# A sixth seven-product unit in the second feed-forward layer of a two-layer encoder, units spread evenly, their first phase bank pair by bank pair, and one more raw and split weight buffer

## The chip, the cores and the metric

The kernel runs on one core of one Trainium2 chip. The metric is the device time of one execution in microseconds, as the median of several. TensorE (PE; its weight loads are PEld) multiplies, VectorE (DVE) and ScalarE (ACT) work element by element, GpSimd (POOL) here only issues DMAs that add, and SyncE (SP) issues the weight loads.

## The reference

Two encoder layers on x of 256 tokens x 2048 channels, all float32. The first has a mixer of pooling and grouped-query attention, the second a bidirectional mLSTM. Each is followed by the gated feed-forward part that this change is about:

```python
D_FF = 5632

def conv_ffn(x, w_up, conv_w, conv_b, w_down):
    u = x @ w_up                                  # 2048 -> 2 * D_FF
    up = jnp.pad(u, ((0, 0), (1, 1), (0, 0)))
    u = c[0] * up[:, :-2] + c[1] * up[:, 1:-1] + c[2] * up[:, 2:] + conv_b
    gate, val = jnp.split(u, 2, axis=-1)
    return (jax.nn.silu(gate) * val) @ w_down

x = x + conv_ffn(rms_norm(x, norm_ffn[layer]), w_up[layer], conv_w[layer], conv_b[layer], w_down[layer])
```

## The kernel before

**Weights as a stream.** All weights of the program stand in one list of chunks, mostly 128 x 1024 floats (512 KB). `Stream.load` has SP load chunk i into a raw tile `w{i}`. `Stream.split` makes a pair `hl{i}` of it: a cast to the rounded type by ScalarE (line 152) and the remainder by VectorE (line 153). TensorE then multiplies three times (high x high, high x low, low x high). Tiles come from pools of a fixed number of buffers, and chunk i + n waits in the queue of ScalarE until TensorE has let go of the buffer of chunk i. Inside a feed-forward layer there are `wraw` 6 + 1 raw and `wsplit` 4 + 1 split buffers (`home` gives every seventh or fifth chunk the extra one); `la` and `sa` say how many chunks ahead are loaded and split.

**A feed-forward layer.** The 44 feature tiles of 128 (each has a gate and a value half) are made in blocks c = 0 to 5 of 4, 8, 8, 8, 8 and 8 tiles (`FCH`). A plain tile `up` takes 4 chunks and 64 matmuls: 32 of 512 columns and 32 of 256. A *unit* makes four tiles at once: the product of 2 x 2 blocks (two halves of the tokens, two halves of a pair of weight rows) by seven products in place of eight, into four PSUM banks `p1`, `p5`, `p6`, `p4`. It takes 16 chunks in its first phase (8 weight quadrant sets p, each with a chunk for p1 and p5 and one for p6 and p4), then 8 chunks for p5 and p6 with one more for p1 after every second: 28 in all, and 7 x 8 x 3 matmuls of 512 columns. Then the banks are combined (lines 1047 to 1068: c12, c21, c22, c11), and `finish` transposes them back tile by tile (line 1081, four transposes a tile), at 3, 7, 11 and 15 us of the planner's clock after the unit's last chunk. `tail` does for every tile the convolution (lines 958 to 961), SiLU (964), the product with the value half (965), and writes the tile to `g` in a high part (966, ScalarE) and a low part (967, VectorE). The sums of weight quadrants that a unit needs are made ahead of time for kinds 1 to 3 by DMAs that add in DRAM (`make_step`, lines 121 to 128: two copies by SP and four accumulates by POOL for a quad of kind 2); the rest, and all of kind 0, are made by VectorE in `sums` (lines 140 to 146).

The down-projection `dn{layer}_{c}_{b}` multiplies block c's tiles in `g`, k = 0 to 7, two a chunk, with four column blocks b, and adds into x. Block c's down-projection is interleaved with block c + 1.

**What sets the order.** `UNITS` lists for each layer the units as (block, half, first slot, last slot, kind), and `_ffn_plan` lays their chunks between the slots of the plain tiles and of the down-projection. TensorE's order is this program order. ScalarE's, VectorE's and SP's come from a scheduler at build time; each queue is then fixed. `late` keeps a unit from taking its banks until the `finish` of the one before is written.

Of the kernel before, what the change touches and what calls it, by code (L numbers as in the profile page):

```python
# [16 lines left out]
P = 128  # L17
# [47 lines left out]
class Stream:  # L65
# [152 lines left out]


@with_exitstack  # L220
def trunk(ctx: ExitStack, tc: tile.TileContext, gx, xT, xn, call, catt, cml, weights, make, out):
# [239 lines left out]
    def attention_layer(norm, nxt):  # L461
        with ExitStack() as es:
# [475 lines left out]
    def ffn_layer(layer, norm, nxt):  # L938
        with ExitStack() as es:
# [76 lines left out]
            def sum_of(j, p):  # L1016
                return [sx[:, j, p, i, :] for i in range(2)]

            def quads(fs, c, i0, name):

                def bank(j):
                    return psp.tile([P, 512], F32, tag="ps", name=f"p{j}_{name}")

# [4 lines left out]
                r0, r1 = norm.rcol[:, 0:1], norm.rcol[:, 1:2]  # L1028
                for p in range(m):
                    ends = p == 0, p == m - 1  # L1030
                    if p == 0:
                        wv.until(lambda: not late)
                        late.update((0, 2))
                    hl = st.next()
                    if p == 0:
                        b1, b5 = bank(1), bank(5)
                    product(b1, block_of(2 * p, 0), hl, 0, *ends)
                    product(b5, sum_of(0, p), hl, 512, *ends)
                    yield
                    hl = st.next()  # L1040
                    if p == 0:
                        b6, b4 = bank(6), bank(4)
                    product(b6, sum_of(1, p), hl, 0, *ends)
                    product(b4, block_of(2 * p + 1, 1), hl, 512, *ends)
                    if p == m - 1:
                        c12, c21, c22 = part(12), part(21), part(22)
                        a.activation(c12, b1, AF.Copy, scale=n0)
                        a.activation(c21, b1, AF.Copy, scale=r1)
                        a.activation(c22, b5, AF.Copy, scale=r1)
                        v.scalar_tensor_tensor(c12, b6, n0, c12, ALU.mult, ALU.add)  # L1050
                    yield
# [22 lines left out]
            def finish(top, bottom, fs, gt, i0, name):  # L1074

                for n, f in enumerate(fs):
                    tr = psp.tile([P, 2, S], F32, tag="ps", name=f"tr{layer}_{f}")
                    for j in range(2):
# [67 lines left out]
            gts, run, late = {}, {}, set()  # L1146
            def g_of(c):
                if c not in gts:
                    gts[c] = actp.tile([P, 8, 2, S], F32R, tag=f"B{c % 2}", name=f"g{layer}_{c}")
                return gts[c]  # L1150

            for step in _ffn_plan(layer):
                kind, c = step[:2]
                key = step[:3]
                if key not in run:
                    f0 = sum(FCH[:c])
                    run[key] = (up(f0 + step[2], g_of(c), step[2]) if kind == "n" else
                                down(c, gts[c], step[2]) if kind == "d" else
                                quads([f0 + 4 * step[2] + j for j in range(4)], c, 4 * step[2], f"{layer}_{c}{step[2]}"))
# [3 lines left out]
            st.la, st.sa, st.more = 5, 2, None  # L1163

# [60 lines left out]
def _down_chunks(w):  # L1225
# [56 lines left out]
def _ffn_order(layer, up, dn, four, last):  # L1282
# [4 lines left out]
    for step in _ffn_plan(layer):  # L1287
# [7 lines left out]
        else:  # L1295
            u = [e[:2] for e in UNITS[layer]].index((c, i))
            made = UNITS[layer][u][4]
            if n >= 2 * m and (n - 2 * m) % 3 == 2:
                seq.append(last[u, (n - 2 * m) // 3])
                continue  # L1300
            at = n // 2 if n < 2 * m else (n - 2 * m) // 3 * 2 + (n - 2 * m) % 3
            q, key = four[u, at], f"{layer}{c}{i}_{at}"
            if n >= 2 * m:
                seq.append(("made", ((key, 1, 2), q[:, 1024:1536])) if made == 1 else ("left", q[:, 512:1536]))
            elif n % 2:
                seq.append(("made", ((key, 2, 4),)) if made in (1, 2) else ("chain", q[:, 1024:2048]))
# [127 lines left out]
```

## Time and profile before

| | |
|---|---|
| median of 3 runs | 2161.71 us (2161.03 to 2166.64) |
| profiled execution, span from first to last instruction | 2160.9 us |
| attention layer, until the first `up` | 256.4 us |
| first feed-forward layer | 712.3 us |
| mLSTM layer | 479.7 us |
| second feed-forward layer, 1448.4 to the last matmul | 708.2 us |
| TensorE busy | 2153.2 us |

The page gives no other time of the profiled execution than its span; the median of the runs stands 0.8 us above it, which is what lies around the span. The layers are cut where the chain in order of time shows their first and last matmuls. The shares of busy time on a page are averages: a stage with an idle engine beside one that is full is read from windows of the trace, and a wait from the row of the instruction that was late, which names in brackets how long its engine was idle and who ended it.

### The profile page before, as it was taken

What the parts mean: (1) busy time and instruction counts of PE and PEld (TensorE: products, weight loads), DVE (VectorE), ACT (ScalarE), POOL (GpSimd) and SP (SyncE); (2) the same over time, 40 slices, a digit from 0 to 9 for tenths busy, and PEclk for the clock granted to TensorE, in tenths of its full rate; (3) what the DMA queues carried; (4) which work ended last, traced back from release to release, by engine and by line L of the source; (5) the groups of instructions that cost most, each with busy time, mean ns of one, the idle gap of its engine ahead of it and who ended that gap; (6) DMA issues with size and microseconds to landing.
All of it is one profiled execution on the core that took longest, in us unless ns stands there. A gap on an engine that the chain in (4) does not pass through costs nothing.

```text
span 2160.9 us, 31049 instructions
## 1 busy us (share of the span) xinstructions
PE 2153.2 (100%) x10896; PEld 1826.7 (85%) x10896; DVE 1717.8 (79%) x2400; ACT 1309.2 (61%) x1840; POOL 276.0 (13%) x344
## 2 busy tenths in 40 slices
PE   9999999999999999999999999999999999999999
PEld 7888888888888888888888888888888888888887
DVE  7686698989889797866777677669898888879785
ACT  7665566766557576655454544556676666757663
POOL 0122111111111111111111111110000010000000
PEclk9999999999999999999999999999999999999999
DMA  8878899999999999979998998887999999877773
GB/s 325 257 229 246 256 262 345 316 332 320 308 325 308 351 332 339 319 200 250 250 263 251 256 253 244 258 244 223 312 286 306 302 297 288 272 249 238 259 245 119
DMA packets 204702, 596.15 MB, mean 276 GB/s; under 512 B 26010, under 2 KB 28354, under 8 KB 204546
## 3 DMA queue, kind: packets, MB, share of 16 engines
q1 hardware_dynamic: 167776, 531.43, 70.1%
q0 software_dynamic: 33696, 59.00, 18.3%
q10 hardware_dynamic: 3074, 3.75, 0.9%
q8 instruction: 85, 1.39, 0.2%
q14 instruction: 71, 0.58, 0.1%
HBM read 591.93 MB, written 119.58 MB: 329 GB/s over the span
## 4 chain that ended last, share of the span: by engine, by line
PE 93%; DMA 5%; DVE 1%; ACT 0%; issue 0%; SPq 0%; ACTq 0%; DVEq 0%
PE up L268 23%; PE dn L268 20%; PE p L268 16%; PE op L268 8%; PE mo L268 4%; PE mk L268 4%; PE mq L268 4%; PE mv L268 3%; PE qproj L268 3%; PE kproj L268 1%; PE vproj L268 1%; PE tr L1081 1%; DMA w<-G 1%; PE pool L268 1%; DMA w<-in_m_in 1%; DMA w<-in_up 1%
## 5 line engine op out<-in xcount | busy, mean ns | idle before, releaser
L153 DVE TENSOR_TENSOR hl<-w,hl 128x1024 fp32r<-128x1024 f32 (+2 forms) x892 | 1075.6, 1218 | 319.9 <-ACT hl L152 302.0
L152 ACT CAST hl<-w 128x1024 fp32r<-128x1024 f32 (+2 forms) x891 | 924.8, 1048 | 646.9 <-PE up L268 98.9
L268 PE MATMUL up<-xx,hl 128*128 128x512 f32 (+1 forms) x3072 | 560.2, 337 | 0.0
L268 PEld LDWEIGHTS up<-xx,hl 128*128 128x128 f32 x3072 | 486.7, 188 | 76.7
L268 PE MATMUL dn<-hl,g 128*128 128x512 f32 x2064 | 491.8, 391 | 0.0
L268 PEld LDWEIGHTS dn<-hl,g 128*128 128x128 f32 x2064 | 385.1, 188 | 79.0
L268 PE MATMUL p<-hl,sx 128*128 128x512 f32 x960 | 250.6, 390 | 0.0
L124 POOL DMA_DIRECT2D G<-in_q x160 | 132.0, 830 | 875.5 <-DMA G<-in_q 872.4
L268 PEld LDWEIGHTS p<-hl,sx 128*128 128x128 f32 x960 | 176.0, 188 | 34.4 <-DVE hl L153 0.6
L128 POOL DMA_DIRECT2D G<-G x144 | 127.9, 888 | 538.2 <-DMA G<-in_q 243.0
L268 PE MATMUL p<-hl,xx 128*128 128x512 f32 x720 | 193.5, 390 | 0.0
L268 PEld LDWEIGHTS p<-hl,xx 128*128 128x128 f32 x720 | 130.8, 188 | 24.0
L268 PE MATMUL mk<-xx,hl 128*128 128x512 f32 (+1 forms) x512 | 92.5, 338 | 1.4 <-DVE hl L153 1.4
L268 PE MATMUL mq<-xx,hl 128*128 128x512 f32 (+1 forms) x512 | 92.2, 337 | 0.0
L268 PE MATMUL mv<-hl,xx 128*128 128x512 f32 (+2 forms) x480 | 91.8, 350 | 0.0
L268 PE MATMUL op<-hl,cat 128*128 128x512 f32 x384 | 91.6, 393 | 0.0
L268 PE MATMUL mo<-hl,xx 128*128 128x512 f32 x384 | 90.5, 391 | 0.0
L268 PEld LDWEIGHTS mk<-xx,hl 128*128 128x128 f32 x512 | 79.0, 188 | 13.1 <-DVE hl L153 1.8
L268 PE MATMUL op<-hl,mcat 128*128 128x512 f32 x384 | 89.5, 392 | 0.0
L268 PEld LDWEIGHTS mq<-xx,hl 128*128 128x128 f32 x512 | 79.3, 188 | 11.6
L268 PEld LDWEIGHTS mv<-hl,xx 128*128 128x128 f32 x480 | 78.3, 189 | 11.2
L268 PEld LDWEIGHTS op<-hl,mcat 128*128 128x128 f32 x384 | 71.5, 188 | 14.6
(242 smaller groups left out, 1865.2 us busy)
## 6 DMA issues: line engine op xcount, KB each, us to landing
w<-in_up SPq DMA_DIRECT2D x192, 512.0 KB, 6.1
w<-in_dn SPq DMA_DIRECT2D x176, 512.0 KB, 6.2
w<-in_m_in SPq DMA_DIRECT2D x124, 512.0 KB, 6.0
w<-in_q SPq DMA_DIRECT2D x88, 512.0 KB, 6.2
G<-in_q SPq DMA_DIRECT2D x144, 256.0 KB, 6.4
G<-G POOLq DMA_DIRECT2D x144, 256.0 KB, 7.5
w<-G SPq DMA_DIRECT2D x72, 512.0 KB, 6.1
w<-in_a_in SPq DMA_DIRECT2D x46, 512.0 KB, 6.1
```

The costliest lines, as they stand in the source:

```text
L124: pin(add.dma_start(G[r, 0:512], src[r, 512:1024], accum_op=ALU.add))
L128: pin(add.dma_start(G[:, at : at + 512], G[:, of : of + 512], accum_op=ALU.add))
L152: (self.nc.vector.tensor_copy if i + c == 0 else self.nc.scalar.copy)(hl[:, 0, c : c + n], w[:, c : c + n])
L153: self.nc.vector.tensor_sub(hl[:, 1, c : c + n], w[:, c : c + n], hl[:, 0, c : c + n].bitcast(F32))
L268: pe.matmul(out_, lhsT, rhs, start=start, stop=stop, skip_group_check=True)
L1081: pe.transpose(tr[:, j, t * P : t * P + P], src[:, c : c + P], ident)
```

## The change

The second layer's block 3 has now both of its halves as units: (3, 0) is new, of kind 2. The six units there follow each other with a pause of 1.5 slots, where the five had pauses of 7 slots. From block 4 on, the plain tiles of a block come ahead of the down-projection of the block before. Units of kinds 1 and 2, in both layers, run all eight chunks of p1 and p5 first, then all eight of p6 and p4 (`apart`); the PSUM pool of four banks is two pools of two, with p1 and p5 on one side, and p6, p4 and the transposes on the other. Every raw and split pool has one more buffer, and `la` and `sa` are one higher everywhere; the DMA scratch of the program is 4096 bytes a partition to make room. The last 20 quads (they were 12) of the second layer are made 12 chunks apart, each within 15 chunks, instead of 17 apart and within 24.

```diff
     def home(self, i, raw):
-        return ((self.wpool if i % 7 < 6 else self.more[0]) if raw else
-                (self.spool if i % 5 < 4 else self.more[1]))
+        return ((self.wpool if i % 8 < 7 else self.more[0]) if raw else
+                (self.spool if i % 6 < 5 else self.more[1]))
...
+class Banks:
+    def __init__(self, *pools):
+        self.pools, self.n = pools, 0
+
+    def tile(self, shape, dtype, tag, name, side=None):
+        if side is None:
+            side = self.n % 2
+            self.n += 1
+        return self.pools[side].tile(shape, dtype, tag=tag, name=name)
...
-    wp = pool("wraw", 6)
-    sp = pool("wsplit", 4)
+    wp = pool("wraw", 7)
+    sp = pool("wsplit", 5)
...
-    psp = pool("ps", 4, space=PSUM)
+    psp = Banks(pool("ps", 2, space=PSUM), pool("pq", 2, space=PSUM))
...
-            st.sa = 2
+            st.la, st.sa = 6, 3
...
-                for p in range(m):
+                for q in range(2 * m):
+                    p, second = (q % m, q >= m) if apart else (q // 2, q % 2)
                     ends = p == 0, p == m - 1
-                    if p == 0:
+                    if q == (m if apart else 0):
                         wv.until(lambda: not late)
                         late.update((0, 2))
                     hl = st.next()
-                    if p == 0:
-                        b1, b5 = bank(1), bank(5)
-                    product(b1, block_of(2 * p, 0), hl, 0, *ends)
-                    product(b5, sum_of(0, p), hl, 512, *ends)
-                    yield
-                    hl = st.next()
+                    if not second:
+                        if p == 0:
+                            b1, b5 = bank(1), bank(5)
+                        product(b1, block_of(2 * p, 0), hl, 0, *ends)
+                        product(b5, sum_of(0, p), hl, 512, *ends)
+                        yield
+                        continue
...
-            st.la, st.sa, st.more = 7, 3, (lp(f"fw{layer}", 1), lp(f"fh{layer}", 1), st.at + len(_ffn_plan(layer)))
+            st.la, st.sa, st.more = 8, 4, (lp(f"fw{layer}", 1), lp(f"fh{layer}", 1), st.at + len(_ffn_plan(layer)))
...
-    ((1, 1, 17, 39, 2), (2, 1, 46, 67, 2), (3, 1, 74, 97, 2), (4, 1, 104, 128, 2), (5, 1, 135, 157, 2)),
+    ((1, 1, 17, 37, 2), (2, 1, 38.5, 59, 2), (3, 0, 60.5, 80, 2), (3, 1, 81.5, 99, 2), (4, 1, 100.5, 123, 2),
+     (5, 1, 124.5, 146, 2)),
...
+            if c > 3 and len(UNITS[layer]) > 5:
+                fill.sort(key=lambda e: e[0] == "d")
...
-    nc = _bacc.Bacc("TRN2", target_bir_lowering=False, num_devices=1)
+    nc = _bacc.Bacc("TRN2", target_bir_lowering=False, num_devices=1, dynamic_dma_scratch_size=4096)
...
-                  + [(at + 17 * k, 8) for k in range(12)])
+                  + [(at + 12 * k, 5) for k in range(20)])
```

In the rows of the order that follow, `p1_1_41` is bank p1 of unit (4, 1) of the second layer, `dn1_3_0` the first column block of block 3's down-projection, `hl792` the split pair of chunk 792, `y1_25` and the cast to `g1_3` behind it feature tile 25, which is k = 5 of block 3 (24 is k = 4; both belong to unit (3, 1)). The changed file's lines stand 13 to 16 higher from `mm` on.

TensorE, before, at the begin of block 3's down-projection; k = 4 and 5 come with its third chunk, hl768:

```order
L268 MATMUL p6_1_41_17107<-hl763_17171,sx1_13321 128x512 x3
L268 MATMUL p4_1_41_17108<-hl763_17171,xx3_9017 128x512 x3
L268 MATMUL dn1_3_0_17240<-hl764_17182,g1_3_15913 128x512 x12
L268 MATMUL p1_1_41_17094<-hl765_17220,xx3_9017 128x512 x3
L268 MATMUL p5_1_41_17095<-hl765_17220,sx1_13321 128x512 x3
L268 MATMUL dn1_3_0_17240<-hl766_17231,g1_3_15913 128x512 x12
L268 MATMUL p6_1_41_17107<-hl767_17243,sx1_13321 128x512 x3
L268 MATMUL p4_1_41_17108<-hl767_17243,xx3_9017 128x512 x3
L268 MATMUL dn1_3_0_17240<-hl768_17261,g1_3_15913 128x512 x12
```

ScalarE, before, where tiles 24 and 25 are cast to g:

```order
L152 CAST hl761_17139<-w761_17064 128x1024
L966 CAST g1_3_15913<-y1_24_16990 128x256
L964 ACTIVATE y1_25_17043<-y1_25_17043 128x256
L152 CAST hl762_17150<-w762_17088 128x1024
L152 CAST hl763_17171<-w763_17102 128x1024
L966 CAST g1_3_15913<-y1_25_17043 128x256
L152 CAST hl764_17182<-w764_17115 128x1024
```

Both casts stood behind the casts of chunks up to hl763, five chunks ahead of hl768.

TensorE at the same place in the change; the third chunk is hl792:

```order
L281 MATMUL dn1_3_0_17629<-hl788_17540,g1_3_16484 128x512 x12
L281 MATMUL p1_1_41_17427<-hl789_17569,xx3_9029 128x512 x3
L281 MATMUL p5_1_41_17428<-hl789_17569,sx1_13332 128x512 x3
L281 MATMUL dn1_3_0_17629<-hl790_17609,g1_3_16484 128x512 x12
L281 MATMUL p1_1_41_17427<-hl791_17620,xx3_9029 128x512 x3
L281 MATMUL p5_1_41_17428<-hl791_17620,sx1_13332 128x512 x3
L281 MATMUL dn1_3_0_17629<-hl792_17632,g1_3_16484 128x512 x12
L281 MATMUL p6_1_41_17712<-hl793_17650,sx1_13332 128x512 x3
```

ScalarE in the change, where tiles 24 and 25 are cast to g:

```order
L152 CAST hl796_17692<-w796_17630 128x1024
L1062 ACTIVATE c12_1_41_17871<-p1_1_41_17427,n0_1_13333 128x512
L1063 ACTIVATE c21_1_41_17872<-p1_1_41_17427,re_n3_13411 128x512
L152 CAST hl797_17709<-w797_17647 128x1024
L1064 ACTIVATE c22_1_41_17873<-p5_1_41_17428,re_n3_13411 128x512
L971 ACTIVATE y1_25_17556<-tb_1_25_17554,cst_87 128x256 x2
L979 CAST g1_3_16484<-y1_24_17501 128x256
L971 ACTIVATE y1_31_17592<-tb_up1_31_17588,cst_87 128x256 x2
L977 ACTIVATE y1_25_17556<-y1_25_17556 128x256
L977 ACTIVATE y1_31_17592<-y1_31_17592 128x256
L979 CAST g1_3_16484<-y1_25_17556 128x256
```

The casts to g for hl792 stand now behind copies of p1 and p5, whose last first-phase products are hl791's, and behind the cast of hl797, five chunks past hl792. Split buffers are six in turn here (hl791 and hl797 have the same one) and were five before. VectorE in the change, at the end of that place:

```order
L153 TENSOR_TENSOR hl797_17709<-w797_17647,hl797_17709 128x1024
L972 SCALAR_TENSOR_TENSOR y1_25_17556<-tb_1_25_17554,cst_87,y1_25_17556 128x255 x2
L980 TENSOR_TENSOR g1_3_16484<-y1_24_17501,g1_3_16484 128x256
L974 SCALAR_TENSOR_TENSOR y1_25_17556<-tb_1_25_17554,cst_87,y1_25_17556 128x255 x2
L972 SCALAR_TENSOR_TENSOR y1_31_17592<-tb_up1_31_17588,cst_87,y1_31_17592 128x255 x2
L974 SCALAR_TENSOR_TENSOR y1_31_17592<-tb_up1_31_17588,cst_87,y1_31_17592 128x255
L978 TENSOR_TENSOR y1_25_17556<-y1_25_17556 128x256
L974 SCALAR_TENSOR_TENSOR y1_31_17592<-tb_up1_31_17588,cst_87,y1_31_17592 128x255
L978 TENSOR_TENSOR y1_31_17592<-y1_31_17592 128x256
L980 TENSOR_TENSOR g1_3_16484<-y1_25_17556,g1_3_16484 128x256
```

The low part of tile 25 has moved behind the split of hl797 and behind plain tile 31.

The second place is the last down-projection of the layer. TensorE in the change, where unit (5, 1) has ended and its last tile (41, k = 5) is transposed inside `dn1_5_0`'s first chunk:

```order
L281 MATMUL dn1_5_0_19336<-hl886_19232,g1_5_18134 128x512 x6
L1096 MATMUL tr1_41_19348<-cst_87,c11_1_51_19173 128x128
L1096 MATMUL tr1_41_19348<-cst_87,c21_1_51_18811 128x128
L1096 MATMUL tr1_41_19348<-cst_87,c11_1_51_19173 128x128
L1096 MATMUL tr1_41_19348<-cst_87,c21_1_51_18811 128x128
L281 MATMUL dn1_5_0_19336<-hl886_19232,g1_5_18134 128x512 x6
L281 MATMUL dn1_5_0_19336<-hl887_19249,g1_5_18134 128x512 x12
L281 MATMUL dn1_5_0_19336<-hl888_19284,g1_5_18134 128x512 x12
```

ScalarE behind these transposes, in the change:

```order
L1098 COPY tb_1_41_19353<-tr1_41_19348 128x512
L971 ACTIVATE y1_41_19355<-tb_1_41_19353,cst_87 128x256 x2
L152 CAST hl892_19391<-w892_19282 128x1024
L152 CAST hl893_19408<-w893_19317 128x1024
L977 ACTIVATE y1_41_19355<-y1_41_19355 128x256
L979 CAST g1_5_18134<-y1_41_19355 128x256
```

Before, a whole plain tile (39) and a column block of `dn1_4` stood between these transposes and `dn1_5_0`; now its third chunk, hl888, needs tile 41.

The third place is VectorE at the begin of the mLSTM layer, where `arg0` waits for a DMA through DRAM. Before:

```order
L153 TENSOR_TENSOR hl420_9471<-w420_9380,hl420_9471 128x1024
L801 COPY mc_9444<-cols_9439 128x8 x8
L829 SCALAR_TENSOR_TENSOR arg0_9578<-G0_9575,mc_9444,kml_9028 128x128
L829 SCALAR_TENSOR_TENSOR arg0_9578<-G0_9575,mc_9444,kml_9028 128x256 x2
L829 SCALAR_TENSOR_TENSOR arg0_9578<-G0_9575,mc_9444,kml_9028 128x128
```

In the change:

```order
L153 TENSOR_TENSOR hl421_9479<-w421_9388,hl421_9479 128x1024
L814 COPY mc_9456<-cols_9451 128x8 x8
L842 SCALAR_TENSOR_TENSOR arg0_9586<-G0_9583,mc_9456,kml_9040 128x128
L842 SCALAR_TENSOR_TENSOR arg0_9586<-G0_9583,mc_9456,kml_9040 128x256 x2
L842 SCALAR_TENSOR_TENSOR arg0_9586<-G0_9583,mc_9456,kml_9040 128x128
```

One split more stands ahead of it.

More of the change, by code (lines that the diff above doesn't have):

```diff
@@ L1017, in sum_of, with quads @@
                 return [sx[:, j, p, i, :] for i in range(2)]
-            def quads(fs, c, i0, name):
+            def quads(fs, c, i0, name, apart):
                 def bank(j):
-                    return psp.tile([P, 512], F32, tag="ps", name=f"p{j}_{name}")
+                    return psp.tile([P, 512], F32, tag="ps", name=f"p{j}_{name}", side=int(j in (1, 5)))
                 def part(j):
@@ L1076, in finish @@
                 for n, f in enumerate(fs):
-                    tr = psp.tile([P, 2, S], F32, tag="ps", name=f"tr{layer}_{f}")
+                    tr = psp.tile([P, 2, S], F32, tag="ps", name=f"tr{layer}_{f}", side=0)
                     for j in range(2):
@@ L1158, in ffn_layer @@
                                 down(c, gts[c], step[2]) if kind == "d" else
-                                quads([f0 + 4 * step[2] + j for j in range(4)], c, 4 * step[2], f"{layer}_{c}{step[2]}"))
+                                quads([f0 + 4 * step[2] + j for j in range(4)], c, 4 * step[2], f"{layer}_{c}{step[2]}",
+                                      (c, step[2]) in apart))
                 next(run[key], None)
@@ L1162, in ffn_layer @@
                 assert next(e, None) is None
-            st.la, st.sa, st.more = 5, 2, None
+            st.la, st.sa, st.more = 6, 3, None
     norms = [Norm(0), None]
@@ L1300, in _ffn_order @@
                 continue
-            at = n // 2 if n < 2 * m else (n - 2 * m) // 3 * 2 + (n - 2 * m) % 3
+            second = n >= m if made in (1, 2) else n % 2
+            at = (n - 2 * m) // 3 * 2 + (n - 2 * m) % 3 if n >= 2 * m else n % m if made in (1, 2) else n // 2
             q, key = four[u, at], f"{layer}{c}{i}_{at}"
```

3 lines of the change are left out of this document (2 added, 1 removed).

## The prediction

> **What bounds the kernel now.** I read the page first: engine totals, TensorE clock, shares of the chain.
>
> ```profile
> span 2160.9 us, 31049 instructions
> ...
> PE 2153.2 (100%) x10896; PEld 1826.7 (85%) x10896; DVE 1717.8 (79%) x2400; ACT 1309.2 (61%) x1840; POOL 276.0 (13%) x344
> ...
> PEclk9999999999999999999999999999999999999999
> ...
> PE 93%; DMA 5%; DVE 1%; ACT 0%; issue 0%; SPq 0%; ACTq 0%; DVEq 0%
> ```
>
> TensorE is busy all the time at its full clock, and the chain that ended last is 93% TensorE. So the time is the sum of TensorE's work, plus the places where it waits. Whether the second feed-forward layer has such places is read from the windows of the two layers (columns: stretch, its length, busy time of PE, PEld, DVE, ACT, POOL, granted clock, DMA share, GB/s).
>
> ```profile
> 1448.40:2156.60 708.20, 708.20 (x3523) 598.73 (x3521) 595.01 (x780) 444.38 (x577) 38.94 (x48) 1.00 0.82 262
> 256.40:968.70 712.30, 711.58 (x3548) 601.24 (x3547) 612.53 (x813) 456.90 (x604) 111.67 (x139) 1.00 0.99 312
> ```
>
> The second layer (first row) has no idle TensorE at all, though VectorE works 84% of it (595.01 of 708.20). A matmul removed there is a gain, if nothing that it covered comes late.
>
> **The change part by part. Matmuls.** Four `up` tiles give way to one unit. Two long stretches of the chain in order of time give the pace, and the groups by form show that `p` and `dn` matmuls are alike.
>
> ```profile
> 266.76 41.10 PE up L268 x236
> ...
> 2102.19 43.53 PE dn L268 x192
> ```
>
> ```profile
> L268 PE MATMUL dn<-hl,g 128*128 128x512 f32 x2064 | 491.8, 391 | 0.0
> ...
> L268 PE MATMUL p<-hl,sx 128*128 128x512 f32 x960 | 250.6, 390 | 0.0
> L268 PEld LDWEIGHTS p<-hl,sx 128*128 128x128 f32 x960 | 176.0, 188 | 34.4 <-DVE hl L153 0.6
> ```
>
> Removed: 4 x 64 matmuls at 41.10/236 = 0.174 us, 44.6 us. Added: 7 x 8 x 3 = 168 at 43.53/192 = 0.227 us, 38.1 us, and four groups of four transposes. A group in the timeline (start, length, what):
>
> ```profile
> 2084.95 0.60 PE L1081 MATMUL tr<-cst,c 128*128 128x128 f32 x4
> 2085.31 4.38 PE L268 MATMUL dn<-hl,g 128*128 128x512 f32 x18
> ```
>
> The next matmul starts 0.36 us after the transposes, and its row is 0.13 us longer than 17 spacings and one matmul of 0.39 (4.25): 0.5 us each, 1.9 us for four. Sum: 44.6 - 38.1 - 1.9 = **-4.6 us**.
>
> **VectorE and ScalarE.** A unit takes 28 weight chunks for the 16 of four `up` tiles, and 8 of them are summed first.
>
> ```profile
> L153 DVE TENSOR_TENSOR hl<-w,hl 128x1024 fp32r<-128x1024 f32 x882 | 1067.2, 1222 | 316.4 <-ACT hl L152 298.5 <-DMA G<-in_q 3.7 <-DMA w<-in_m_in 2.4
> L152 ACT CAST hl<-w 128x1024 fp32r<-128x1024 f32 x882 | 918.0, 1051 | 643.9 <-PE up L268 98.9 <-PE dn L268 93.2 <-DVE w L140 90.5
> ...
> L140 DVE TENSOR_TENSOR w<-w 128x512 f32<-128x512 f32 x80 | 54.8, 685 | 1.6 <-DMA w<-in_q 1.6
> ```
>
> VectorE gets 12 x 1.22 + 8 x 0.69 = 20.1 us more; the combining of banks it adds and the gathering of `up` it drops are within 2 us of each other. So about 615 us in 704: 87%, against 86% (612.53 of 712.30) in the first layer, which lost 0.7 us of TensorE. On average this is hidden; the question is where work that TensorE needs soon stands in the queue.
>
> **The wait at block 3's down-projection.** Here the order rows of the change decide. From unit (3,1)'s last chunk to the third chunk of `dn1_3_0` TensorE's rows, counted at the paces above, take 32 us now and took 49 before. In ScalarE's order the casts of g tiles 24 and 25, which `dn1_3_0` reads with chunk hl792, stand behind three copies that need unit (4,1)'s last first-phase products (chunk hl791) and behind the cast of hl797. There are six split buffers, so hl797 takes the buffer of hl791; that such casts wait for TensorE to let go of a buffer is the row of L152 above (98.9 us for `up`, 93.2 for `dn`). So these casts can't be done before TensorE has finished hl791, and hl792 is TensorE's very next row: it must wait. The durations:
>
> ```profile
> L1047 ACT ACTIVATE c<-p,n x10: 673/682/686, 352.8 to 2029.9; 128x512 f32<-128x512 f32 x10
> L1048 ACT ACTIVATE c<-p,re_n x10: 673/682/690, 353.4 to 2030.4; 128x512 f32<-128x512 f32 x10
> L1049 ACT ACTIVATE c<-p,re_n x10: 681/694/702, 354.0 to 2032.0; 128x512 f32<-128x512 f32 x10
> ```
>
> ```profile
> 2106.96 1.10 ACT L958 ACTIVATE y<-tb_up,cst 128x256 f32<-128x256 f32 x2 [0.94 <-DVE tb_up L977]
> ...
> 2107.96 0.40 ACT L964 ACTIVATE y<-y 128x256 f32<-128x256 f32 x1
> 2108.27 1.04 ACT L152 CAST hl<-w 128x1024 fp32r<-128x1024 f32 x1
> ```
>
> Queued back to back, each next one starts 0.1 us before the end shown (2106.96 + 1.10 against 2107.96). Let 0 be TensorE's start on hl791. The cast of hl796, freed by hl790, runs from 0.2 to 1.2. Then c12 0.6, c21 0.6, cast hl797 0.95, c22 0.6, two activations 1.0, cast of g24 0.4: done at 5.4. TensorE is due at 6 x 0.227 = 1.4, so it waits 4.0. Its k = 4 matmuls end at 6.8. VectorE meanwhile has the second half of split hl797 (cast ends at 3.4, then 1.2), two steps of tile 25, the low part of g24, and then, ahead of g25, five more conv steps of 0.40 and a product; after them ScalarE casts g25 (0.4):
>
> ```profile
> L961 DVE SCALAR_TENSOR_TENSOR y<-tb,cst,y 128x255 f32<-128x255 f32 x80 | 36.3, 479 | 0.0
> L966 ACT CAST g<-y 128x256 fp32r<-128x256 f32 x88 | 35.3, 401 | 4.2 <-DVE y L965 4.2
> L967 DVE TENSOR_TENSOR g<-y,g 128x256 fp32r<-128x256 f32 x88 | 36.8, 419 | 0.2 <-ACT g L966 0.2
> ```
>
> Low g24 at 5.9, conv steps to 7.9, product 8.3, cast 8.75, low part 9.4: k = 5 waits 1.9 and 0.2 more. Sum 6.1; with VectorE a little behind I take **+6.5**. Lower end: ScalarE's row alone (two activations, two SiLUs and a cast, 1.9 us, behind 5.4 - 0.1, against 6.8): 4.0 + 0.4 = 4.4. Upper end: if VectorE comes in without any lead. From split hl779 to g25 it has 18 splits at 1.14 back to back and 16.2 us of tails and bank sums, 36.7 us, and TensorE's rows there are 27.4 us: 9.
>
> **The wait at the last down-projection.** Only six `dn` chunks (16 us) now stand between unit (5,1) and `dn1_5_0`; the last transposes (tile 41) go into its first chunk. Before, tile 41's way looked so (transposes; cast of g):
>
> ```profile
> 2099.49 0.60 PE L1081 MATMUL tr<-cst,c 128*128 128x128 f32 x4
> ...
> 2111.36 0.40 ACT L966 CAST g<-y 128x256 fp32r<-128x256 f32 x1
> ```
>
> 11.9 us, most of it behind casts that wait for buffers. Now g41 is needed 1.36 + 2.72 + 1.36 = 5.4 us after the transposes, and it stands behind the cast of hl893, which waits for hl887: free at 4.1, cast from 4.3 to 5.35, SiLU 0.3 and split 1.2 (to 6.55), product 0.4, cast 0.4: 7.4. **+2.0**; ends 1.0 (VectorE takes the product ahead in time) and 3.0 (one more split).
>
> **The spare buffers.** The split lookahead is one chunk longer outside the layers too. One wait of TensorE sits in the mLSTM layer's begin:
>
> ```profile
> 1012.21 0.35 DVE L829 SCALAR_TENSOR_TENSOR arg<-G,mc,kml 128x128 f32<-128x128 f32 x1 [2.51 <-DMA G<-gd]
> ...
> 1016.56 1.66 PE L268 MATMUL mk<-xx,hl 128*128 128x256 f32 x8 [1.38 <-DVE hl L153]
> ```
>
> VectorE stood at L829 for a DMA, with the next split behind it. In the order rows one more split (hl421) now stands ahead of it, 2.8 us of matmuls: **-1.4** (ends 0 and -1.4). In the first layer one wait is left:
>
> ```profile
> 767.53 4.12 ACT L152 CAST hl<-w 128x1024 fp32r<-128x1024 f32 x4 [2.62 <-DMA w<-in_b]
> ...
> 776.42 0.55 PE L1081 MATMUL tr<-cst,c 128*128 128x128 f32 x3 [0.72 <-DVE c L1058]
> ```
>
> It begins with a late load; one more raw buffer gives 2 us: **-0.7** (ends 0 and -0.7).
>
> Phase order, bank sides and spread are costed at nothing: each phase still has a fill chunk between most of its own, TensorE waited for `p` banks nowhere, and two fill chunks (5.5 us) stand between one unit's last b1 product and the next one's first, against c11's copy of some 0.69 (as L1049). Ends: 0 and +1.
>
> **DMA.** The queues of the page:
>
> ```profile
> q1 hardware_dynamic: 167776, 531.43, 70.1%
> q0 software_dynamic: 33696, 59.00, 18.3%
> ```
>
> That is 2.85 us per MB and 6.7 us per MB. The unit brings 12 loads of 0.52 MB (18 us) and eight made quads, each with 0.79 MB copied and 0.79 MB accumulated (60 us): (0.82 x 708 + 78)/704 = 0.94, below the first layer's 0.99. Cost 0, ends 0 and +2.
>
> ```profile
> L124 POOL DMA_DIRECT2D G<-in_q x160 | 132.0, 830 | 875.5 <-DMA G<-in_q 872.4 <-issue 3.0
> ```
>
> ```profile
> G<-G POOLq DMA_DIRECT2D x144, 256.0 KB, 7.5
> ```
>
> No row shows the smaller descriptor scratch. POOL waits for the copies that it adds to and hardly for its own issuing (3.0 us), so 0. At the other end every accumulate would wait for the landing of the one before: 4 x 7.5 = 30 us a quad, planned every 12 chunks (25 us); 20 quads run 100 us late, 30 more than the 34 chunks (70 us) of lead: +30. I leave it outside the range, with 0.02 in rival 3. [...]
>
> The sum from the profiled execution (2160.9): -4.6 + 6.5 + 2.0 - 1.4 - 0.7 = +1.8, 2162.7; the median of the runs shown is 0.8 above that span, so **2163.5 us**.
>
> A rule stands behind the two waits. They rest on ScalarE and VectorE taking their queue in order. The row at 1012.21 shows it: a split whose data was there stayed behind L829, and TensorE sat idle. [...]
>
> **Rivals.** (1) *Slower: VectorE idles in the stretch of n40 to n43.* From split hl751 to g25 it has 84.0 us of work by its order rows, in 84.6 us of TensorE's. Usually it idles (316.4 us before L153, nearly all for ScalarE's cast). If 7% of the stretch goes so, 6 us, the wait at hl792 is 12.5 instead of 6.5, and the time 2169.5. It decides when more than about 5 us are lost. For it: VectorE waits for a cast 301 times. Against: the first row below, a stretch as full that cost TensorE nothing.
>
> ```profile
> 1620.00:1640.00 20.00, 20.00 (x94) 16.70 (x93) 19.93 (x31) 15.11 (x21) 1.64 (x2) 1.00 0.95 294
> ```
>
> (2) *Faster: the waits don't come*, as ScalarE gets to g24 and g41 in time: 2161.7 - 6.7 = 2155.0, -0.3%. Against: the order itself. (3) *Loads late:* the first 250 chunks hold 20 quads of 7.5 us and 250 loads of 1.5, 525 us of DMA in 513 us of TensorE's; if the 12 us over that the lookahead of eight raw buffers (some 17 us) doesn't hold, a third of it shows, +4: 2167.5. Against: 0.99 over the whole first layer. (4) *The change doesn't do what it says:* TensorE isn't relieved because the unit's matmuls wait for splits; then -4.6 falls away and the time is 2168. Against: no `p` matmul waits in 10 units, but for the 0.6 us of the PEld row above.
>
> **How the numbers follow.** Forecast 0.64, (1) 0.13, (2) 0.07, (3) 0.11, (4) 0.05. What a measurement tells from no change is about 0.3%, 6.5 us: faster is below 2155.2, slower above 2168.2. Faster: most of (2) and a little of the forecast's edge, 0.08. Slower: (1), half of (4) and some of (3), 0.17. Same: 0.75. The forecast's bounds (4.4 to 9 and 1 to 3, recoveries gone or not, +2 for loads) give 2160 to 2168.5; with part of (1) and (2) 2157.0 to 2169.5.
>
> **What would show it.** Right: two idle places on TensorE in the second layer, of 5 to 8 us in two pieces at the third chunk of `dn1_3_0` (some 1900 us in), released by ScalarE's g cast, and of 2 us some 45 us before the end; the wait at `mk` gone; 168 more `p` matmuls; VectorE near 87% of the layer. Wrong: no idle place at `dn`, waits of `p` or `up` on splits (rivals 1 and 4), or casts waiting for loads (3).

## The result, and the profile after

The changed kernel takes 2166.34 us (median of 13 runs, 2165.36 to 2168.32), the kernel before 2160.45 us (13 runs, 2159.77 to 2166.64): a ratio of 1.0026, with an interval of 1.0019 to 1.0033. It is slower by 5.9 us. That is clear of the interval, but under the 0.3% from which the prediction would have called it slower (2168.2 us). The prediction said 2163.5, within 2157.0 to 2169.5.

The page of the changed kernel, its totals, its chain, and two of its groups (line, engine, operation, tile, form, count; busy us and mean ns; idle time just before and who ended it):

```profile
span 2164.0 us, 31051 instructions
...
PE 2152.8 (99%) x10824; PEld 1822.8 (84%) x10824; DVE 1734.3 (80%) x2417; ACT 1321.4 (61%) x1856; POOL 301.6 (14%) x376
...
PE 99%; DVE 1%; issue 0%; ACT 0%; DVEq 0%; ACTq 0%
...
L281 PE MATMUL dn<-hl,g 128*128 128x512 f32 x2064 | 495.7, 392 | 6.3 <-ACT g L979 6.3
...
L281 PE MATMUL p<-hl,sx 128*128 128x512 f32 x1056 | 280.8, 391 | 0.0
```

TensorE's share fell from 100% to 99%. All of its new idle time stands in one group: the down-projection waits 6.3 us for ScalarE's cast of `g`, which was 0.0 before. The unit's own matmuls (`p`) wait for nothing.

Where it lies is read from windows (stretch, its length, then busy time of PE, PEld, DVE, ACT, POOL, granted clock of TensorE with 1.00 as full speed, DMA share, GB/s):

```profile
256.00:970.00 714.00, 714.00 (x3570) 604.31 (x3569) 615.53 (x818) 459.33 (x610) 113.37 (x141) 1.00 0.99 311
970.00:1100.00 130.00, 130.00 (x762) 115.06 (x762) 92.17 (x151) 71.15 (x98) 23.25 (x29) 1.00 0.94 257
...
1800.00:2000.00 200.00, 195.50 (x933) 163.07 (x932) 166.87 (x209) 126.08 (x161) 17.31 (x22) 0.97 0.92 296
```

The first layer and the mLSTM layer's begin have no idle TensorE left. From 1800 to 2000 it idles 4.5 us, and the granted clock is 0.97. The forecast had the idle time; it had nothing about the clock. TensorE's timeline there, from the chunk ahead of hl792 (start, length, what, count, idle time before and releaser):

```profile
1909.21 0.84 PE L281 MATMUL p<-hl,sx 128*128 128x512 f32 x3
1913.79 3.16 PE L281 MATMUL dn<-hl,g 128*128 128x512 f32 x6 [3.73 <-ACT g L979]
1917.71 2.93 PE L281 MATMUL dn<-hl,g 128*128 128x512 f32 x6 [0.76 <-ACT g L979]
1920.44 1.48 PE L281 MATMUL p<-hl,sx 128*128 128x512 f32 x3
1921.72 1.48 PE L281 MATMUL p<-hl,xx 128*128 128x512 f32 x3
1923.00 1.10 PE L281 MATMUL p<-hl,sx 128*128 128x512 f32 x3
1923.94 0.85 PE L281 MATMUL p<-hl,xx 128*128 128x512 f32 x3
1924.63 0.61 PE L281 MATMUL dn<-hl,g 128*128 128x512 f32 x2
```

Two waits for ScalarE's cast of `g`, as forecast. But look at the rows behind them: three `p` matmuls take 1.28 us from one row to the next (1920.44 to 1921.72), 0.427 each; at 1923.94 it is 0.69, 0.23 each. From 1909.21 to 1924.63 stand 27 matmuls, 6.1 us at 0.227, in 15.4 us: **9.3 us lost**. Of these 3.9 are standing still in the first wait (1913.79 less 1909.21 and three matmuls) and 1.0 in the second (the 0.76 shown, and 0.2 by which a row at this pace runs past the next one's start: 1.48 against 1.28); the other 4.4 are matmuls at half pace, as rows of 0.427 us a matmul are called from here on. The granted clock of the same stretch:

```profile
1909.90:1913.79 3.89, 0.15 (x1) 0.00 (x1) 3.89 (x6) 3.84 (x7) 0.79 (x1) 0.93 1.05 362
1913.79:1916.60 2.81, 2.81 (x6) 1.67 (x6) 2.81 (x8) 1.40 (x3) 0.00 (x0) 0.50 1.02 399
1916.60:1917.71 1.11, 0.35 (x1) 0.00 (x1) 1.00 (x4) 0.71 (x2) 0.00 (x0) 0.50 1.08 330
1917.71:1923.40 5.69, 5.69 (x13) 4.38 (x14) 2.39 (x4) 1.61 (x3) 0.82 (x1) 0.50 0.52 121
1923.40:1926.00 2.60, 2.60 (x13) 2.12 (x12) 1.31 (x2) 1.94 (x2) 0.84 (x1) 0.98 0.72 206
```

If the clock fell once, 0.93 over the wait of 3.89 us is a clock of 0.5 for the last 0.5 us of it; it stays at 0.50 until 1923.4 and a little more.

ScalarE in the wait is the queue that the prediction counted: the cast that waits for a buffer, the bank copies, the cast of hl797, two activations, and only then the cast to `g`:

```profile
1908.73 1.06 ACT L152 CAST hl<-w 128x1024 fp32r<-128x1024 f32 x1 [0.50 <-PE dn L281]
1909.69 0.68 ACT L1062 ACTIVATE c<-p,n 128x512 f32<-128x512 f32 x1
1910.27 0.67 ACT L1063 ACTIVATE c<-p,re_n 128x512 f32<-128x512 f32 x1
1910.84 1.04 ACT L152 CAST hl<-w 128x1024 fp32r<-128x1024 f32 x1
1911.77 0.69 ACT L1064 ACTIVATE c<-p,re_n 128x512 f32<-128x512 f32 x1
1912.35 1.09 ACT L971 ACTIVATE y<-tb,cst 128x256 f32<-128x256 f32 x2
1913.34 0.40 ACT L979 CAST g<-y 128x256 fp32r<-128x256 f32 x1
```

The last down-projection:

```profile
2116.73 4.72 PE L281 MATMUL dn<-hl,g 128*128 128x512 f32 x20
2123.26 5.08 PE L281 MATMUL dn<-hl,g 128*128 128x512 f32 x21 [1.82 <-ACT g L979]
```

20 matmuls take 4.5 us at 0.227, and the next row starts 6.5 us after the first: 2.0 us of standing still, without a row at half pace behind it (21 matmuls in 5.08).

### The profile page after: what moved, and what is told of

Read it like the earlier page. It is cut to its first block, busy times and chain, and to the rows that moved or that the text cites. A ratio compares the mean times of both kernels' runs of the same rounds, so it can differ in the third digit from the quotient of the medians.

```text
span 2164.0 us, 31051 instructions
## 1 busy us (share of the span) xinstructions
PE 2152.8 (99%) x10824; PEld 1822.8 (84%) x10824; DVE 1734.3 (80%) x2417; ACT 1321.4 (61%) x1856; POOL 301.6 (14%) x376
## 3 DMA queue, kind: packets, MB, share of 16 engines
q8 instruction: 84, 1.38, 0.2%
## 4 chain that ended last, share of the span: by engine, by line
PE 99%; DVE 1%; issue 0%; ACT 0%; DVEq 0%; ACTq 0%
PE up L281 23%; PE dn L281 21%; PE p L281 19%; PE op L281 8%; PE mv L281 4%; PE mq L281 4%; PE mk L281 4%; PE mo L281 4%; PE qproj L281 3%; PE kproj L281 1%; PE pool L281 1%; PE vproj L281 1%; PE tr L1096 1%; PE av L281 1%; PE qk L281 1%; PE end L281 1%
## 5 line engine op out<-in xcount | busy, mean ns | idle before, releaser
L153 DVE TENSOR_TENSOR hl<-w,hl 128x1024 fp32r<-128x1024 f32 (+1 forms) x904 | 1089.3, 1217 | 307.7 <-ACT hl L152 290.5
L152 ACT CAST hl<-w 128x1024 fp32r<-128x1024 f32 (+2 forms) x903 | 936.2, 1048 | 634.6 <-PE dn L281 106.2
L281 PE MATMUL up<-xx,hl 128*128 128x512 f32 (+1 forms) x2816 | 514.4, 337 | 0.0
L281 PEld LDWEIGHTS up<-xx,hl 128*128 128x128 f32 x2816 | 446.9, 188 | 70.7
L281 PE MATMUL p<-hl,sx 128*128 128x512 f32 x1056 | 280.8, 391 | 0.0
L124 POOL DMA_DIRECT2D G<-in_q x176 | 147.6, 840 | 802.3 <-DMA G<-in_q 795.4
L281 PEld LDWEIGHTS p<-hl,sx 128*128 128x128 f32 x1056 | 194.1, 188 | 37.2
L128 POOL DMA_DIRECT2D G<-G x160 | 140.4, 881 | 602.4 <-DMA G<-in_q 285.1
L281 PE MATMUL p<-hl,xx 128*128 128x512 f32 x792 | 217.0, 391 | 0.0
L281 PEld LDWEIGHTS p<-hl,xx 128*128 128x128 f32 x792 | 145.0, 188 | 27.3
```

What stands on the lines that cost most here:

```text
L124: pin(add.dma_start(G[r, 0:512], src[r, 512:1024], accum_op=ALU.add))
L128: pin(add.dma_start(G[:, at : at + 512], G[:, of : of + 512], accum_op=ALU.add))
L152: (self.nc.vector.tensor_copy if i + c == 0 else self.nc.scalar.copy)(hl[:, 0, c : c + n], w[:, c : c + n])
L153: self.nc.vector.tensor_sub(hl[:, 1, c : c + n], w[:, c : c + n], hl[:, 0, c : c + n].bitcast(F32))
L281: pe.matmul(out_, lhsT, rhs, start=start, stop=stop, skip_group_check=True)
```

## The experiments

The theory to be tested: the two forced waits, the first with the half pace behind it, cost 11.3 us and eat what the unit and the buffers gain. Against it: the sixth unit costs by its load on VectorE and the DMA queues wherever it stands; the phase order, the banks or the scratch cost by themselves; the half pace has another cause than the wait. Medians, and the ratio to the kernel before in the same series (2160.38 us of 29 runs for the first four, 2160.22 of 27, on another chip, for the others):

| kernel | us, median (range) | ratio, interval |
|---|---|---|
| before + scratch (e_scratch) | 2160.38 (2160.02 to 2162.01) | 0.9999, 0.9990 to 1.0008 |
| before + buffers (e_spare) | 2159.21 (2159.12 to 2160.10) | 0.9994, 0.9985 to 1.0002 |
| change with five units (e_five) | 2159.62 (2159.39 to 2159.89) | 0.9995, 0.9987 to 1.0004 |
| change, no wait (e_both_gone) | **2154.57** (2154.45 to 2154.79) | 0.9970, 0.9960 to 0.9981 |
| change, last wait alone (e_first_gone) | 2157.05 (2156.62 to 2158.29) | 0.9985, 0.9976 to 0.9994 |
| change, block 3's wait alone (e_last_gone) | 2163.41 (2162.53 to 2163.80, one disturbed run of 4265.34 left out) | 1.0013, 1.0004 to 1.0022 |
| wait in short pieces (e_short_pieces) | 2165.74 (2161.87 to 2166.45) | 1.0023, 1.0012 to 1.0034 |
| one longer wait (e_one_piece) | 2166.13 (2165.05 to 2167.37) | 1.0026, 1.0016 to 1.0036 |

**The parts around the unit.** First the scratch alone, in the kernel before:

```diff
-    nc = _bacc.Bacc("TRN2", target_bir_lowering=False, num_devices=1)
+    nc = _bacc.Bacc("TRN2", target_bir_lowering=False, num_devices=1, dynamic_dma_scratch_size=4096)
```

> The kernel before with nothing changed but the DMA scratch of 4096 bytes. Every theory that costs the scratch at nothing: within 1 us of before, ratio 0.9995 to 1.0005, and a profile like that of before. If each accumulate waited for the landing of the one before, POOL's idle time before L124 and L128 would grow by hundreds of us and the time by up to 30 us. The profile is also a second look at before's own waits: the one at mk of the mLSTM layer (1.38 us) and the one of the first layer (0.72 us) should be there again; if they are missing or shorter, the profiled execution of before was a poor one and the gain of the spare buffers is smaller than its trace says.

No cost of the scratch is seen. Its profile shows the order of before in another execution. The same two windows of the profiled execution of before, and then of this one:

```profile
256.00:970.00 714.00, 713.28 (x3560) 602.90 (x3559) 613.79 (x816) 458.16 (x606) 111.67 (x139) 1.00 0.99 312
970.00:1100.00 130.00, 128.62 (x756) 113.68 (x755) 91.65 (x154) 71.33 (x101) 23.21 (x29) 1.00 0.92 255
```

```profile
256.00:970.00 714.00, 714.00 (x3563) 603.52 (x3562) 614.76 (x816) 458.13 (x606) 111.96 (x139) 1.00 0.99 312
970.00:1100.00 130.00, 130.00 (x765) 115.23 (x764) 92.46 (x154) 71.93 (x102) 23.42 (x30) 1.00 0.91 257
```

TensorE's 0.7 and 1.4 us of idle time, on which the gain of the buffers was counted, are not there: the second case of the expectation. In nearly all runs here a run's time is its span + 1.7 to 2.1 us, mostly 1.8, so by estimate the profiled execution of before (span 2160.9) took some 2162.7, 2.3 more than the median; two later runs of that kernel with the span 2160.9 took 2162.65 and 2162.69.

Then the buffers and the lookahead, still with the old units (the scratch makes room):

```diff
-        return ((self.wpool if i % 7 < 6 else self.more[0]) if raw else
-                (self.spool if i % 5 < 4 else self.more[1]))
+        return ((self.wpool if i % 8 < 7 else self.more[0]) if raw else
+                (self.spool if i % 6 < 5 else self.more[1]))
...
-    wp = pool("wraw", 6)
-    sp = pool("wsplit", 4)
+    wp = pool("wraw", 7)
+    sp = pool("wsplit", 5)
...
-            st.sa = 2
+            st.la, st.sa = 6, 3
...
-            st.la, st.sa, st.more = 7, 3, (lp(f"fw{layer}", 1), lp(f"fh{layer}", 1), st.at + len(_ffn_plan(layer)))
+            st.la, st.sa, st.more = 8, 4, (lp(f"fw{layer}", 1), lp(f"fh{layer}", 1), st.at + len(_ffn_plan(layer)))
...
-            st.la, st.sa, st.more = 5, 2, None
+            st.la, st.sa, st.more = 6, 3, None
...
-    nc = _bacc.Bacc("TRN2", target_bir_lowering=False, num_devices=1)
+    nc = _bacc.Bacc("TRN2", target_bir_lowering=False, num_devices=1, dynamic_dma_scratch_size=4096)
```

> The kernel before with the one more raw and split buffer and the longer lookahead alone (and the smaller scratch that makes room): old units, old phase order, one bank pool. Theory (forced waits in the second layer eat the gain): this part is a gain of its own, 1.4 us at mk and 0.7 us in the first layer, up to 3.1 us as the two profiled executions stand at the begin of the second layer: 2157.4 to 2158.4 us, TensorE without idle places in the second layer, clock 1.00 there. Rival (the edits around the unit cost by themselves, among them the longer lookahead): at or above the 2160.5 us of before.

1.2 us faster than before, where 2 to 3 were expected, and the interval still holds no change at all. And the change with the five units of before, so with the phase order and bank sides:

```diff
-    ((1, 1, 17, 37, 2), (2, 1, 38.5, 59, 2), (3, 0, 60.5, 80, 2), (3, 1, 81.5, 99, 2), (4, 1, 100.5, 123, 2),
-     (5, 1, 124.5, 146, 2)),
+    ((1, 1, 17, 39, 2), (2, 1, 46, 67, 2), (3, 1, 74, 97, 2), (4, 1, 104, 128, 2), (5, 1, 135, 157, 2)),
...
-                  + [(at + 12 * k, 5) for k in range(20)])
+                  + [(at + 17 * k, 8) for k in range(12)])
```

> The change with the five units, slots and making of quads of the second layer that before has; phase order, the two bank pools, spare buffers and scratch stay. Theory (waits): phase order and banks cost nothing, so the same as the spare buffers alone within 1 us, 2157.4 to 2159 us, no idle place at dn and no half pace in the second layer. Rival (the phase order or the bank sides cost): 2 us or more above the spare buffers alone, with waits at p or tr matmuls in both feed-forward layers.

0.4 us above the buffers alone: phase order and banks cost next to nothing. The time is a little above what was expected, since the buffers brought less. This kernel also has the order of before from block 4 on, because the code puts the plain tiles ahead of the down-projection only in a layer with more than five units.

**The waits.** Both are taken away by moving two units in their slots, with the same matmuls, loads and VectorE work:

```diff
-    ((1, 1, 17, 37, 2), (2, 1, 38.5, 59, 2), (3, 0, 60.5, 80, 2), (3, 1, 81.5, 99, 2), (4, 1, 100.5, 123, 2),
-     (5, 1, 124.5, 146, 2)),
+    ((1, 1, 17, 37, 2), (2, 1, 38.5, 59, 2), (3, 0, 60.5, 80, 2), (3, 1, 81, 96, 2), (4, 1, 100.5, 123, 2),
+     (5, 1, 124.5, 143, 2)),
```

> The change with two units moved in their slots alone: (3,1) ends three slots earlier, so that the casts of g24 and g25 stand five chunks earlier in ScalarE's order, and (5,1) ends three slots earlier, so that its last tile is done two dn chunks sooner. Same matmuls, same weights, same VectorE work. Theory (the two waits, 9.2 us at block 3 with the half pace behind it and 2.0 us at the end): both are gone, 2166.3 - 11.2 = 2155.1 us, clock 1.00 in the second layer, TensorE idle nowhere; 4 to 5 us below the change with five units. Rival (the sixth unit's 20 us of VectorE work and its transfers cost wherever they stand): the waits move elsewhere and the time stays at 2164 to 2167 us.

2154.57 us, 11.8 below the change and 5.8 below the kernel before: the fastest kernel here. Two of its windows:

```profile
1600.00:1800.00 200.00, 200.00 (x961) 167.76 (x960) 177.17 (x228) 135.18 (x175) 25.96 (x32) 1.00 1.00 325
1800.00:2000.00 200.00, 200.00 (x983) 168.78 (x982) 174.64 (x222) 134.10 (x173) 17.85 (x22) 1.00 0.94 307
```

VectorE is 89% busy and the DMA engines at 1.00 for 200 us, and TensorE is not idle: the load of the sixth unit is hidden. Against the change with five units it gains 5.05 us. That difference holds, beside the unit, what goes with it: the plain tiles ahead of the down-projection, the slots and the making of the quads; these were not tried apart. Each wait by itself: first only (3, 1) is moved,

```diff
-    ((1, 1, 17, 37, 2), (2, 1, 38.5, 59, 2), (3, 0, 60.5, 80, 2), (3, 1, 81.5, 99, 2), (4, 1, 100.5, 123, 2),
+    ((1, 1, 17, 37, 2), (2, 1, 38.5, 59, 2), (3, 0, 60.5, 80, 2), (3, 1, 81, 96, 2), (4, 1, 100.5, 123, 2),
```

> The change with unit (3,1) moved from slots 81.5 to 99 to slots 81 to 96: the casts of g24 and g25 stand ahead of the copies of unit (4,1); the wait at the last down-projection is left as it is. Theory: 9.2 us less than the change, of which about 5.9 us are TensorE standing still and about 3.3 us the half pace behind it: 2157.1 us, one idle place of 2 us some 40 us before the end. Rival (the half pace has another cause than the wait, as a throttle by time or by load): the matmuls of 0.43 us stay somewhere in the second layer, and the gain is 6 us: 2160.4 us.

and then only the end of (5, 1):

```diff
-     (5, 1, 124.5, 146, 2)),
+     (5, 1, 124.5, 143, 2)),
```

> The change with unit (5,1) ending at slot 143 in place of 146, so that two more dn chunks stand between it and the last down-projection; the wait at block 3 is left. Theory: 2.0 us less than the change, 2164.3 us; the place at block 3 as before, with its half pace. Rival (TensorE's 2 us there are hidden by what comes after, the end being set by the last norm or the output): no change, 2166.3 us.

With (3, 1) moved the time is 9.3 us less than the change, with (5, 1) ending earlier 2.9 less. The wait at block 3 costs what its rows gave, 9.3 us, though their split is 4.9 of standing still and 4.4 of half pace, not the 5.9 and 3.3 of the expectation. The half pace goes with the wait. The same window of the kernel with (3, 1) moved, to be held against the 195.50 and 0.97 of the change:

```profile
1800.00:2000.00 200.00, 200.00 (x983) 168.76 (x982) 174.75 (x223) 134.34 (x173) 17.06 (x21) 1.00 0.94 305
```

With (5, 1) ending earlier, the place at block 3 is as it was (TensorE busy for 195.49 of the 200.00 us and a clock of 0.97 in that window). The last wait costs 2.9 (or 2.5, from 2157.05 to 2154.57), more than its 2.0 of standing still.

**The clock.** The next kernel breaks the wait at block 3 into pieces:

```diff
-    ((1, 1, 17, 37, 2), (2, 1, 38.5, 59, 2), (3, 0, 60.5, 80, 2), (3, 1, 81.5, 99, 2), (4, 1, 100.5, 123, 2),
+    ((1, 1, 17, 37, 2), (2, 1, 38.5, 59, 2), (3, 0, 60.5, 80, 2), (3, 1, 81.5, 99, 2), (4, 1, 100.5, 120, 2),
```

> The change with unit (4,1) ending at slot 120 in place of 123. In the order the down-projection's third chunk (hl794) now waits for g24 behind the cast of hl798 alone, and g25 stands behind one more cast, a SiLU and two activations: TensorE idles about as long in all, 5 to 6 us, but in pieces of about 2 us with matmuls between them. Theory (the half pace comes from one idle stretch of some 4 us; 2 us, as at the last down-projection, do not bring it): no matmuls of 0.43 us, clock 1.00 outside the idle pieces, 2166.3 - 3.3 = 2163 us, up to 1 us less if the pieces are shorter. Rival (the clock answers to the summed idle time): the half pace is there, 2166 us.

The expectation failed. The pieces are there, and the clock falls all the same. TensorE's timeline, and the clock before, in and behind the rows at half pace:

```profile
1914.54 0.73 PE L281 MATMUL dn<-hl,g 128*128 128x512 f32 x2 [1.36 <-ACT g L979]
1916.83 1.20 PE L281 MATMUL dn<-hl,g 128*128 128x512 f32 x4 [1.56 <-DVE g L980]
1919.13 3.15 PE L281 MATMUL dn<-hl,g 128*128 128x512 f32 x6 [1.10 <-ACT g L979]
```

```profile
1912.80:1919.10 6.30, 2.31 (x8) 0.97 (x6) 6.30 (x12) 4.44 (x8) 0.93 (x2) 0.98 1.02 368
1919.13:1922.10 2.97, 2.97 (x7) 2.00 (x8) 2.27 (x6) 0.82 (x2) 0.54 (x1) 0.50 0.85 281
1922.10:1925.00 2.90, 2.90 (x14) 2.40 (x13) 1.40 (x2) 2.10 (x2) 0.01 (x1) 0.98 0.52 98
```

No piece is longer than 1.6 us by the brackets. Counted from row to row, as above, the three are 1.5, 1.8 and 1.4 us, 4.8 in all, about what the two at block 3 were. This execution took 2163.25 us; six of the eight runs took 2165.4 or more, near the 2166 of the rival. The opposite case is one long wait:

```diff
-    ((1, 1, 17, 37, 2), (2, 1, 38.5, 59, 2), (3, 0, 60.5, 80, 2), (3, 1, 81.5, 99, 2), (4, 1, 100.5, 123, 2),
+    ((1, 1, 17, 37, 2), (2, 1, 38.5, 59, 2), (3, 0, 60.5, 80, 2), (3, 1, 81.5, 99, 2), (4, 1, 100.5, 118, 2),
```

> The change with unit (4,1) ending at slot 118. In the order g24 is cast in time, and g25 stands behind the casts of hl799 and hl800 (the latter free only when TensorE has come to hl794), four activations and two SiLUs: TensorE waits once, for about 5 us, at the third chunk. Theory (one long idle stretch brings the half pace): about 5 to 6 us of standing still and again some 10 us of matmuls at 0.43 us behind it, so 8 to 10 us lost at this place, 2165 to 2167 us. Rival (the half pace was an accident of the transfers or splits behind the first wait): 5 to 6 us lost, 2162 to 2163 us, all matmuls at 0.227 us.

2166.13 us, as expected, and TensorE again ran at half pace, which the rival had ruled out. But in the profiled execution (2165.05 us) it lasted 4.8 us behind the wait, where some 10 were expected. The wait and the clock in it, at half pace, and behind:

```profile
1921.56 2.93 PE L281 MATMUL dn<-hl,g 128*128 128x512 f32 x6 [5.61 <-ACT g L979]
```

```profile
1915.90:1921.50 5.60, 0.05 (x1) 0.00 (x0) 5.51 (x12) 2.63 (x7) 0.82 (x1) 0.82 1.04 391
1921.56:1926.30 4.74, 4.74 (x11) 3.77 (x12) 1.44 (x3) 1.33 (x2) 0.17 (x1) 0.50 0.61 141
1926.30:1930.00 3.70, 3.70 (x17) 3.00 (x17) 2.44 (x3) 2.10 (x2) 0.66 (x1) 0.99 0.55 87
```

The runs with only the last wait (e_first_gone) had fallen into two groups. Two more executions of that kernel were profiled, and one more of the kernel with the short pieces:

> A second look at the kernel with only the last wait (2.0 us). Its 11 runs fell into two groups, six of 2156.6 to 2157.1 us at clock 1.000 and five of 2157.9 to 2158.3, four of these at 0.999. [...] Rival (the groups have to do with transfers or the output): no matmuls of 0.43 us in either, the 1.3 us lie elsewhere.

> The same look once more, since one execution shows only one of the two groups: the time alone says beforehand which, 2157 us without matmuls of 0.43 us behind the wait, 2158.2 with them.

> A second look at the pieces of 1.5 to 2 us. Six of eight runs took 2165.4 to 2166.5 us, two 2161.9 and 2163.3; the profiled one was the latter and had some ten matmuls of 0.43 us. [...] Rival (longer pieces make the difference): the pieces sum to 7 us or more, and the half pace is as short as in the first look.

The two new executions of e_first_gone took 2158.72 and 2158.27 us, the slower group; the one profiled first was of the faster (2156.82). The clock just behind the same wait, in the first execution and then in the second:

```profile
2114.34:2115.10 0.76, 0.76 (x3) 0.60 (x4) 0.41 (x1) 0.00 (x0) 0.00 (x0) 1.00 0.48 151
2115.10:2118.50 3.40, 3.40 (x16) 2.78 (x16) 1.23 (x1) 1.05 (x1) 0.00 (x0) 1.00 0.30 120
```

```profile
2114.65:2115.45 0.80, 0.80 (x3) 0.60 (x4) 0.41 (x1) 0.00 (x0) 0.00 (x0) 0.99 0.61 210
2115.45:2118.85 3.40, 3.40 (x9) 2.65 (x8) 0.79 (x1) 1.04 (x1) 0.00 (x0) 0.50 0.27 105
2118.85:2121.00 2.15, 2.15 (x11) 1.76 (x10) 0.76 (x2) 0.32 (x1) 0.00 (x0) 1.00 0.04 8
```

The same kernel and the same wait of 1.82 us: in one execution no matmul is slow, in the other the clock is 0.50 for 3.4 us: some eight matmuls at 0.427, 1.7 us lost. The third execution (e_first_gone_c) has some eight as well, by a clock of 0.53 over 3.42 us. From the start of the row ahead of the wait to the wait's end it is 4.70 us with 12 matmuls in the first, 4.93 with 13 in the second and 4.47 with 11 in the third: at 0.227 a matmul the same to 0.01 us, so that row doesn't tell them apart. The first ran on another chip than the other two, but its eleven runs there hold both groups. Why the same wait brings the half pace in one execution and not in another is not shown. The half pace accounts for the last wait's 2.5 to 2.9: 2.0 and, in part of the runs, 1.7. The new execution of the short pieces took 2163.32 us, so by its time it is the light case once more (2163.25 in the first). No execution of 2165.4 us or more of that kernel was profiled: a longer half pace in those is not shown, and whether the sum of the idle time decides there stays open.

## Why the prediction came out as it did

The sign of the sum and its mechanism were right: a gain of the unit, eaten by two waits that the order forces. What the forecast had no term for is the half pace behind them. By the medians of the experiments: -1.2 buffers, +0.4 phase order and banks, -5.05 unit, +9.3 and +2.5 waits, together +6.0; measured 5.9.

- **Matmuls, -4.6.** Right: -5.05, with the order, slots and quads that go with the unit. The change has the forecast 168 more `p` matmuls (1056 + 792 against 960 + 720). TensorE's busy time is 2152.59 with five units and 2147.80 with six and no wait.
- **The wait at block 3's down-projection, +6.5 (4.4 to 9).** Right in place, releaser and first piece: 4.0 forecast, 3.9 measured, for the queue it named. This is the term that was mis-sized, at 9.3, above its upper end: it priced the matmuls behind the wait at 0.227 us, and they ran at 0.427 for some 10 us. That cost 4.4. The standing still alone was 4.9, below the 6.1 of the working and just below the 5 to 8 given as a sign. The second piece was 1.0 in place of 2.1; that fits the slow matmuls of k = 4, in whose time ScalarE and VectorE catch up, but no run tries it. In the execution of before that the forecast was read from, the longest wait of TensorE was 1.38 us, and the clock behind it was 1.00 (1016.50 to 1030.00): no row there has a half pace to price.
- **The wait at the last down-projection, +2.0 (1 to 3).** Right for standing still (2.0); 2.5 to 2.9 with the clock.
- **The spare buffers, -1.4 and -0.7.** Too much: 1.2 by medians, and not to be told from none. The two waits were real in the execution that was profiled, but e_scratch's, with the same order, had neither. The step that failed is the one from a single execution to the median. The same step gave the 0.8 us between span and median: it set the median of three runs beside an execution that was itself some 2.3 us slower than most. So the base was 1.3 too high (2161.7 against 2160.4) and the effects 4.1 too low (+1.8 against +5.9), which is the 2.8 between 2163.5 and 2166.3. That the two errors offset each other in part was luck.
- **Phase order, banks, spread: 0 to +1.** 0.4 for the first two; the spread is inside the -5.05 and was not measured by itself. **Scratch: 0.** Right. **DMA: 0.** Right: in e_both_gone its share was 1.00 over 200 us without a wait of TensorE.
- **Rivals.** VectorE's idle time, late loads and matmuls that wait for splits (1, 3 and 4) fall with e_both_gone, which carries the same load with TensorE busy for all of the 552 us from 1448 to 2000 and for 149.03 of the 152.7 behind them, and with the 0.0 of the `p` row; against (1) stands also the first wait itself, 3.9 us where 4.0 were forecast. That the waits don't come (2) falls with the two rows released by ScalarE's cast; e_both_gone shows what it would have been worth, 2154.6 against the 2155.0 forecast.

The rule on queues in order agrees with ScalarE's rows in the wait: the cast to `g` at 1913.34 came behind everything written ahead of it, the cast of hl797 at 1910.84 among it.

## What to carry to other kernels

When a producer moves closer to its consumer, follow the copy that lies between them through its engine's queue, and look for rows ahead of it that wait for a buffer which the consumer's own engine has yet to release. Here two such waits were removed by letting the producers end three slots earlier, with the work kept (2166.34 to 2154.57 us). Price a wait of TensorE with the half pace that may stand behind it (0.427 us a matmul in place of 0.227, here behind a wait of 1.82 us in two of three executions, and behind pieces of 1.36, 1.56 and 1.10 us), and check a wait that is to be gained against several executions before it is counted.

## What the runs showed of the hardware that was not expected

By estimate from the clock of the windows, the half pace lasted 3.4 us or twice or three times that: 3.4 behind the wait of 1.82 us (when it came at all), 10.2 behind the two at block 3 (0.5 in the wait, from the 0.93, and 9.6 to 1923.4, with the 0.98 a little more), 6.8 around the one of 5.61 us (0.82 over 5.60 us is 2.0 us at half, and 4.74), and 3.3 at the short pieces of the first execution (0.98 over 6.30 us is 0.25, then 2.97, and 0.98 over 2.90 is 0.1). In it a matmul of 512 columns took 0.427 us in place of 0.227. It came without a stretch as long as the 3.73 us of block 3: behind pieces of 1.36, 1.56 and 1.10 us in the first execution of e_short_pieces, and behind a single wait of 1.82 us in two of three executions of e_first_gone, but not behind the same wait in the changed kernel (21 matmuls in 5.08 us). What sets its length, and why the same wait brings it in one execution and not in another, was not shown.
